# Experts in pairs, and their rows fetched by indirect DMA instead of gathered by one-hot products

## The chip, the core and the metric

The kernel runs on one core of one Trainium2 chip. The metric is the device time of one execution in microseconds, taken as the median of three runs.

## What is computed

One decoder layer on 512 tokens of 1024 channels in float32: a pooling mixer and multi-head latent attention side by side, an output projection, then a mixture of 32 experts of which each token takes four, and a final norm. The change lies in the mixture:

```python
logits = ht @ w_router + b_router
top_vals, top_idx = lax.top_k(logits, 4)
gates = jax.nn.softmax(top_vals, axis=-1)
...
gu = xblk @ w_gate_up[e] + b_gate_up[e]          # 1024 -> 2048
gate = jnp.minimum(gu[:, :1024], 7.0)
up = jnp.clip(gu[:, 1024:], -7.0, 7.0)
act = gate * jax.nn.sigmoid(1.702 * gate) * (up + 1)
return act @ w_down[e] + b_down[e]               # 1024 -> 1024
...
y = zeros.at[row_tok].add(row_gate[:, None] * yb)
```

All weights of all experts have to be read: 8 MB of gate-and-up and 4 MB of down for each of the 32.

## The kernel before

The first part (projections, attention, mixer, router) ends after about 200 us. Then the experts are worked on at 32 positions, ordered by how many tokens they have, in the pattern `KINDS = "BSSS" + "BS" * 12 + "SSSS"`. A big position (B) takes up to 128 tokens; its weights are split by `split` (L863) into a high part on ACT (L866) and a low part on DVE or POOL (L867), and each product is three passes (`mm3`, L95 to L97, for gate and up; L970 for down). A small position (S) takes up to 64 tokens and multiplies in float32 with two column halves side by side (L910, L992).

For each position the kernel does these steps: `load_expert` puts the weights into a ring of eight 1 MB slots by DMAs on SP's queue, in the order in which positions are worked on (8 slots of gate-and-up, then 4 of down). `select` (L794) makes a one-hot of the position's tokens over its slots on DVE. `gather` (L807) multiplies the normalised rows, kept in two float16 parts `hb`, with that one-hot (L837): 64 matmuls for a position, of 128 columns for B and of 64 for S, whose result already lies with channels on partitions. It is scaled into `xgs` (L848, S), or into `xgh` and `xgl` (L819 and L820, B). `gate_up` (L878) does the products, `act` the activation (`swiglu`, L917, on DVE and ACT), `turn` (L935) transposes it on PE (L949), `slot_info` (L850) gets token number and gate of every slot by the one-hot (L856), `down` (L958) does the second product, and `combine` (L1040) adds the gated rows to the tokens by scatter products (L1051) that a later `gate_up` takes along, one part after each of its steps.

The loop at L1278 runs position after position: gate-and-up of r, activation, the gather for r + 1, turn, down of r. The order on each engine's queue is not quite the program's: a scheduler in the framework lists the instructions of each engine by its own estimate of when they can run, and each engine then works through its list in order. In the list of PE the gate-and-up products of an S stand mixed with the down products of the B before it. PSUM has four banks `gu` for gate-and-up, two banks `d` for down and for half of a gather, and two banks `m` for the rest.

## Time and profile before

| | us |
|---|---|
| time, median of 3 runs (lowest, highest) | 1401.42 (1400.72, 1401.83) |
| profiled execution, first to last instruction (span) | 1392.6 |
| median time less that span | 8.8 |
| PE busy in the span | 1305.3 (94%) |
| DVE busy | 869.9 (62%) |
| ACT busy | 568.8 (41%) |
| POOL busy | 402.1 (29%) |

The profiled execution's own time is not listed apart from its span; what lies around the span is taken as the 8.8 us by which the median exceeds it. PE is the matmul engine, PEld its weight loads, DVE, ACT and POOL the vector, scalar and general engine, SP the engine whose queue issues the weight loads. A busy PE need not be PE at its peak, since matmuls overlap and their ends are modelled. The whole chain of waits is 62% PE. The mean granted clock of PE is 0.974 of 2.4 GHz.

### The profile page before, as it was taken

The numbers are of one execution on the slowest core, as the hardware profiler recorded it, in microseconds if no ns is written. First come the engines' busy times: TensorE is split into PE (matmuls) and PEld (weight loads), VectorE is DVE, ScalarE is ACT, GpSimd is POOL, SyncE is SP. The second block draws the span as 40 slices with busy tenths as digits, with TensorE's granted clock in tenths as the row PEclk, the third lists the DMA queues.
The fourth block names the chain that finished last, engine by engine and source line by source line (L and its number), as shares of the span: only waits on it lengthen the run. The fifth ranks groups of instructions, "written<-read, shape, count | busy, mean of one in ns | idle before, by whom it ended". The sixth has DMA issues, their size and how long they took to land.

```text
span 1392.6 us, 20172 instructions
## 1 busy us (share of the span) xinstructions
PE 1305.3 (94%) x7465; PEld 793.2 (57%) x7465; DVE 869.9 (62%) x1439; ACT 568.8 (41%) x819; POOL 402.1 (29%) x264
## 2 busy tenths in 40 slices
PE   7989988999899999999899999999899999999995
PEld 6756675534547465665657565746566565743432
DVE  6897688334847485675758593748577575832324
ACT  5476554212525263444434452626344444420003
POOL 1445334101514133332323241423333233310001
PEclk9999999999899999999999999999999999999998
DMA  8213417899889797979899898979797989999893
GB/s 300 76 59 105 155 73 257 332 407 373 327 333 334 276 382 274 378 289 367 327 333 355 335 338 320 356 293 380 273 385 287 369 326 359 346 351 399 343 421 138
DMA packets 83265, 422.29 MB, mean 303 GB/s; under 512 B 8729, under 2 KB 8857, under 8 KB 50394
## 3 DMA queue, kind: packets, MB, share of 16 engines
q1 hardware_dynamic: 82964, 420.57, 78.7%
q8 instruction: 60, 0.98, 0.3%
q10 hardware_dynamic: 198, 0.39, 0.1%
q14 instruction: 43, 0.35, 0.1%
HBM read 418.70 MB, written 2.23 MB: 302 GB/s over the span
## 4 chain that ended last, share of the span: by engine, by line
PE 62%; DVE 7%; ACT 2%; issue 1%; DVEq 0%; ACTq 0%
PE gu L910 18%; PE d L970 10%; PE d L992 7%; PE gu L95 5%; PE gu L96 5%; PE gu L97 5%; PE m L1051 5%; PE m L837 3%; DVE mlo L867 2%; DVE au L928 1%; PE m L949 1%; PE d L837 1%; DVE au L927 1%; ACT mhi L866 1%; DVE au L929 1%
## 5 line engine op out<-in xcount | busy, mean ns | idle before, releaser
L867 POOL TENSOR_TENSOR mlo<-slot,mhi 128x1024 fp32r<-128x1024 f32 x116 | 318.1, 2747 | 708.0 <-ACT mhi L866 707.9
L867 DVE TENSOR_TENSOR mlo<-slot,mhi 128x1024 fp32r<-128x1024 f32 x196 | 344.8, 1770 | 97.7 <-ACT mhi L866 95.4
L866 ACT CAST mhi<-slot 128x1024 fp32r<-128x1024 f32 x312 | 320.4, 1051 | 200.2 <-PE gu L97 133.2
L910 PE MATMUL gu<-slot,xgs 128*64 128x512 f32 x1216 | 305.8, 620 | 3.2 <-DVE xgs L848 3.2
L910 PEld LDWEIGHTS gu<-slot,xgs 128*64 128x64 f32 x1216 | 82.9, 140 | 151.7 <-issue 144.2
L96 PE MATMUL gu<-mlo,xgh 128*128 128x512 f32 x416 | 165.8, 399 | 2.9 <-DVE mlo L867 2.7
L97 PE MATMUL gu<-mhi,xgl 128*128 128x512 f32 x416 | 163.0, 393 | 0.0
L992 PE MATMUL d<-slot,ats 128*64 128x512 f32 x576 | 132.6, 609 | 0.0
L95 PE MATMUL gu<-mhi,xgh 128*128 128x512 f32 x416 | 127.5, 397 | 0.0
L926 ACT ACTIVATE as<-ag 128x512 f32<-128x512 f32 x45 | 28.4, 632 | 230.1 <-DVE ag L925 229.9
L837 PEld LDWEIGHTS <-hb 128*128 128x128 f16 x1984 | 83.2, 98 | 62.6 <-issue 62.1
L1052 DVE TENSOR_TENSOR y<-y,m 128x512 f32<-128x512 f32 x112 | 74.9, 681 | 48.0 <-PE m L1051 47.5
L925 DVE TENSOR_SCALAR ag<-gu 128x512 f32<-128x512 f32 x45 | 30.9, 688 | 115.9 <-PE gu L910 107.5
L96 PEld LDWEIGHTS gu<-mlo,xgh 128*128 128x128 f32 x416 | 78.3, 189 | 21.4 <-DVE mlo L867 4.0
L97 PEld LDWEIGHTS gu<-mhi,xgl 128*128 128x128 f32 x416 | 78.5, 189 | 16.1
L95 PEld LDWEIGHTS gu<-mhi,xgh 128*128 128x128 f32 x416 | 76.8, 188 | 18.1 <-issue 1.6
L992 PEld LDWEIGHTS d<-slot,ats 128*64 128x64 f32 x576 | 39.9, 139 | 73.7 <-issue 72.8
L977 DVE SCALAR_TENSOR_TENSOR ybl<-d,sl,ybh 128x512 fp32r<-128x512 f32 x26 | 18.3, 747 | 94.4 <-ACT ybh L976 94.4
L837 PE MATMUL m<-oh,hb 128*128 128x64 f16 (+1 forms) x1600 | 74.9, 200 | 1.0 <-DVE oh L802 0.9
L970 PE MATMUL d<-mhi,ath 128*128 128x512 f32 x208 | 69.4, 415 | 0.3 <-ACT ath L952 0.3
L970 PE MATMUL d<-mhi,atl 128*128 128x512 f32 x208 | 66.7, 401 | 0.0
L970 PE MATMUL d<-mlo,ath 128*128 128x512 f32 x208 | 66.2, 398 | 0.0
(389 smaller groups left out, 1687.8 us busy)
## 6 DMA issues: line engine op xcount, KB each, us to landing
slot<-in_w_gate_up_dram SPq DMA_DIRECT2D x256, 1024.0 KB, 6.9
slot<-in_w_down_dram SPq DMA_DIRECT2D x128, 1024.0 KB, 7.9
wraw<-in_w_in_dram SPq DMA_DIRECT2D x16, 256.0 KB, 5.0
wraw<-in_w_out_dram SPq DMA_DIRECT2D x16, 256.0 KB, 2.6
xtraw<-in_xT_dram SPq DMA_DIRECT2D x8, 256.0 KB, 5.1
y<-in_x_dram SPq DMA_DIRECT2D x4, 512.0 KB, 7.0
out_dram<-o SPq DMA_DIRECT2D x4, 512.0 KB, 2.6
wraw<-in_w_qb_dram SPq DMA_DIRECT2D x4, 256.0 KB, 3.5
```

The lines of the kernel that those rows point to most:

```text
L95: nc.tensor.matmul(out, lhsT=shi, rhs=mhi, start=first, stop=False)
L96: nc.tensor.matmul(out, lhsT=shi, rhs=mlo, start=False, stop=False)
L97: nc.tensor.matmul(out, lhsT=slo, rhs=mhi, start=False, stop=last)
L837: PE.matmul(pb[:, i * n:(i + 1) * n], lhsT=q[:, d * P:(d + 1) * P], rhs=oh[:, t, 0:n], start=(m == 0), stop=(m == len(ops) - 1))
L866: S.copy(hi, src)
L867: eng.tensor_tensor(lo, src, hi.bitcast(F32), op=ALU.subtract)
L910: PE.matmul(banks[c // 2][q:q + 64, :], lhsT=xg[r][:, k, :], rhs=w[:, c * T:(c + 1) * T], start=False, stop=(k == KD - 1))
L925: V.tensor_scalar(g, gb, 7.0, None, op0=ALU.min)
L970: PE.matmul(banks[c], lhsT=a[:, k, :], rhs=b[:, c * T:(c + 1) * T], start=(k == 0 and n == 0), stop=(k == KD - 1 and n == 2))
L992: PE.matmul(db[64 * q:64 * q + 64, :], lhsT=at[:, k, :], rhs=w[:, c * T:(c + 1) * T], start=(k == 0), stop=(k == KD - 1))
L1051: PE.matmul(pb, lhsT=a, rhs=b, start=(i == 0), stop=(i == len(todo) - 1))
L1052: V.tensor_tensor(y[:, t, cs], y[:, t, cs], pb, op=ALU.add)
```

## The change

Three things change together. First, the normalised rows are also written to DRAM (`hrow`, 512 rows of 4 KB, by eight DMAs on POOL's queue, `row_parts`). For a position, `fetch` turns the token numbers of its slots into an index column and issues one indirect DMA on POOL's queue, which brings 128 rows of 4 KB into `xr`, one row to a slot. An S and the S after it (`mate`) share one fetch. Second, `gather` turns `xr` by eight PE transposes of 128x128 for a B or for a pair of S's; the gather products at L837 are gone for all positions but the first. Third, the loop goes by a list of steps: after the first six positions, gate-and-up of two positions (a B and an S, at the end two S's), then both down products. The ring is loaded in the order of that list. Since the activation of the first of a pair has to outlive the next gather, `ath` and `atl` get buffers of their own, and PSUM is now six banks `gu` (down too) and two banks `m`. The other parts (`fetch` four steps ahead, `gather` two steps ahead for a B and one for S's, turn, combine) are generators from which `gate_up` and `down` take a part at each of their steps. In `row_parts` the low float16 part of the first token tile moves from POOL to DVE, and POOL makes the float32 rows. Line numbers move: in the changed kernel L849 is the transpose of the fetched rows, L919 and L1001 are the products of S, L959 is the transpose of the activation, L979 the down product of B, L1058 the scatter products, L865 the slot info, L876 the low part of a split.

```diff
-            if (t, c) in POOLP:
-                part = scr("part")
-                G.tensor_scalar(part, yt, r_, None, op0=ALU.mult)
-                G.tensor_tensor(hb[1][:, t, cs], part, hb[0][:, t, cs], op=ALU.subtract)
-            else:
-                V.scalar_tensor_tensor(hb[1][:, t, cs], yt, r_, hb[0][:, t, cs], op0=ALU.mult, op1=ALU.subtract)
+            V.scalar_tensor_tensor(hb[1][:, t, cs], yt, r_, hb[0][:, t, cs], op0=ALU.mult, op1=ALU.subtract)
+            part = cst.tile([P, T], F32, tag="xk3", name="part3") if t == NT - 1 and c else scr("part")
+            G.tensor_scalar(part, yt, r_, None, op0=ALU.mult)
+            G.dma_start(hrow[t * P:(t + 1) * P, cs], part)
...
+    def fetch(r):
+        idx = mo.tile([P, 1], I32, tag="idx", bufs=2, name="idx")
+        if big(r):
+            V.tensor_scalar(idx, slots[r][:, 5:6], 0.0, None, op0=ALU.max)
+        else:
+            q = mate(r)
+            V.tensor_scalar(idx[0:64], slots[r][0:64, 5:6], 0.0, None, op0=ALU.max)
+            V.tensor_scalar(idx[64:P], slots[r if q is None else q][64:P, 5:6], 0.0, None, op0=ALU.max)
+        rows[r] = hbp.tile([P, D], F32, tag="hb", name="xr")
+        G.indirect_dma_start(out=rows[r], out_offset=None, in_=hrow,
+                             in_offset=bass.IndirectOffsetOnAxis(ap=idx[:, 0:1], axis=0), bounds_check=T - 1,
+                             oob_is_err=False)
...
-        for b in range(nb):
-            pb = bank("d" if b and r != "o" and not big(r - 1) else "m")
-            for i in range(per):
-                d = b * per + i
-                ops = [(q[t], t) for t in range(NT) for q in src]
-                for m, (q, t) in enumerate(ops):
-                    PE.matmul(pb[:, i * n:(i + 1) * n], lhsT=q[:, d * P:(d + 1) * P], rhs=oh[:, t, 0:n],
-                              start=(m == 0), stop=(m == len(ops) - 1))
+        xr = rows.pop(r)
+        for b in range(2):
+            pb = bank("m")
+            for i in range(4):
+                d = 4 * b + i
+                PE.transpose(pb[:, i * P:(i + 1) * P], xr[:, d * P:(d + 1) * P], ident)
...
+    steps = [("gu", 0), ("dn", 0), ("gu", 1), ("gu", 2), ("dn", 1), ("gu", 3), ("dn", 2), ("gu", 4), ("dn", 3),
+             ("gu", 5), ("dn", 4), ("dn", 5)]
+    for r in range(6, E, 2):
+        steps += [("gu", r), ("gu", r + 1), ("dn", r), ("dn", r + 1)]
...
+    for i, (what, r) in enumerate(steps):
+        if i:
+            while loaded < i + 3:
+                load(loaded)
+                loaded += 1
+        ahead = {g: steps.index(("gu", g)) - i for g in groups}
+        for g, n in ahead.items():
+            if n <= (2 if big(g) else 1) and g not in gathered and i > 0:
+                gathered.add(g)
+                gathering = itertools.chain(gathering, later(gather(g), 5 if g == 1 else 1))
+            if n <= 4 and g not in fetched and i > 0:
+                fetched.add(g)
+                arriving = itertools.chain(arriving, arrive(g))
+        if what == "gu":
+            banks = gate_up(r, rest, turned, arriving, gathering)
...
+            us_ = act(r, banks)
+            turned = turn(r, us_)
...
+            down(r, rest, turned, arriving, gathering)
```

How the lists of the engines change is seen at three places. The first is on PE, where the last gate-and-up products of a B end. Before, the list goes on with bias products (L885), then the transposes of B's activation (L949, `au` is the activation, `m` a PSUM bank):

```order
L888 LDWEIGHTS m4b
L888 MATMUL gu<-bias,m4b 64x512
L885 LDWEIGHTS m4b
L885 MATMUL gu<-bias,m4b 128x512
L949 MATMUL m<-ident,au 128x128 x4
L885 LDWEIGHTS m4b
L885 MATMUL gu<-bias,m4b 128x512
L856 LDWEIGHTS oh
```

and with the change, at the same place:

```order
L919 MATMUL gu<-slot,xgs 64x512 x4
L96 MATMUL gu<-mlo,xgh 128x512
L97 MATMUL gu<-mhi,xgl 128x512
L96 MATMUL gu<-mlo,xgh 128x512
L97 MATMUL gu<-mhi,xgl 128x512
L919 MATMUL gu<-slot,xgs 64x512 x4
L959 MATMUL m<-ident,au 128x128 x4
L1058 MATMUL m<-ybh,sc 128x512
L1058 MATMUL m<-ybl,sc 128x512
L919 MATMUL gu<-slot,xgs 64x512 x4
L959 MATMUL m<-ident,au 128x128 x4
```

The transposes of the activation now stand behind products of the S of the pair (L919), which are ready to run, and no gather stands ahead of those.

The second place is on PE too, where B's down products run. Before, the S's gate-and-up products (L910) stand among them:

```order
L910 MATMUL gu<-slot,xgs 64x512 x8
L970 MATMUL d<-mhi,ath 128x512 x2
L970 MATMUL d<-mlo,ath 128x512 x2
L970 MATMUL d<-mhi,atl 128x512 x2
...
L949 MATMUL m<-ident,au 128x128 x4
...
L910 MATMUL gu<-slot,xgs 64x512 x8
```

With the change the S's products come first, with the transposes of a fetched group (L849) among them, and the down products of B (L979) follow:

```order
L919 MATMUL gu<-slot,xgs 64x512 x4
L849 MATMUL m<-ident,xr 128x128 x8
L919 MATMUL gu<-slot,xgs 64x512 x12
L979 MATMUL gu<-mhi,ath 128x512 x2
L959 MATMUL m<-ident,au 128x128 x4
```

The S's gate-and-up products, which filled the gaps between B's down products, now lie ahead of them.

The third place is POOL's list in the pairs, which before held only the splits' low parts after the start:

```order
L1180 MEMSET mblk 64x64
L1212 MEMSET aux 128x32 x4
L1249 MEMSET movb 64x64
L1156 TENSOR_TENSOR bd<-bdraw,bd 32x512 x2
L867 TENSOR_TENSOR mlo<-slot,mhi 128x1024 x115
```

and now has the fetches among them:

```order
L876 TENSOR_TENSOR mlo<-slot,mhi 128x1024 x9
L820 DMA xr<-hrow,idx 128x1024
L876 TENSOR_TENSOR mlo<-slot,mhi 128x1024 x4
L820 DMA xr<-hrow,idx 128x1024
L876 TENSOR_TENSOR mlo<-slot,mhi 128x1024 x5
```

Each fetch stands ahead of four, five or nine low parts, which POOL reaches only once it has issued the fetch.

## Rows read from the trace of the kernel before

**Rows 1.** The page's busy time, share of the span and instructions of each engine.

```profile
PE 1305.3 (94%) x7465; PEld 793.2 (57%) x7465; DVE 869.9 (62%) x1439; ACT 568.8 (41%) x819; POOL 402.1 (29%) x264
```

**Rows 2.** Chain of waits, S's down products of eleven pairs: start us, us, what.

```profile
492.14 5.30 PE d L992 x24
...
1242.46 7.02 PE d L992 x32
```

**Rows 3.** Windows, the ten pairs between: busy us (count) by engine, PEclk, DMA share, GB/s.

```profile
core 0: us, PE busy (x) PEld busy (x) DVE busy (x) ACT busy (x) POOL busy (x), PEclk, DMA share, GB/s
492.00:1242.00 750.00, 722.97 (x4208) 454.42 (x4207) 500.77 (x668) 329.55 (x415) 242.00 (x90) 0.98 0.88 336
```

**Rows 4.** Groups by line, activation's transposes: busy us, mean ns | idle before, releaser.

```profile
L949 PE MATMUL m<-ident,au 128*128 128x128 f32 x180 | 30.9, 298 | 28.6 <-DVE au L929 28.6
```

**Rows 5.** Windows, the first six positions.

```profile
209.00:420.00 211.00, 198.66 (x1181) 105.12 (x1179) 118.70 (x189) 66.05 (x86) 48.75 (x17) 0.97 0.87 338
280.00:310.00 30.00, 29.13 (x182) 12.24 (x184) 11.87 (x24) 3.90 (x6) 0.00 (x0) 1.00 1.00 406
340.00:370.00 30.00, 28.01 (x174) 19.87 (x170) 23.99 (x16) 18.36 (x19) 17.29 (x6) 1.00 0.97 373
```

**Rows 6.** Windows, the last four positions up to the tail.

```profile
1242.00:1355.00 113.00, 106.68 (x623) 39.61 (x623) 30.07 (x64) 9.90 (x16) 0.00 (x0) 0.97 0.96 387
1320.00:1340.00 20.00, 18.48 (x121) 6.68 (x119) 5.54 (x12) 1.22 (x2) 0.00 (x0) 1.00 1.01 427
```

**Rows 7.** Chain of waits: eight S products, B's gather in two halves, S's gather.

```profile
611.70 1.87 PE gu L910 x8
...
713.47 1.73 PE m L837 x29
715.19 1.79 PE d L837 x32
...
1238.63 1.94 PE m L837 x63
```

**Rows 8.** Timeline of PE: start us, us, instruction [idle before, releaser].

```profile
610.27 0.66 PE L949 MATMUL m<-ident,au 128*128 128x128 f32 x4 [1.47 <-DVE au L929]
...
642.82 0.61 PE L949 MATMUL m<-ident,au 128*128 128x128 f32 x4
643.26 0.60 PE L885 MATMUL gu<-bias,m4b 96*128 96x512 bf16 x2
```

**Rows 9.** The page's DMA issues: count, KB each, us to landing.

```profile
slot<-in_w_gate_up_dram SPq DMA_DIRECT2D x256, 1024.0 KB, 6.9
slot<-in_w_down_dram SPq DMA_DIRECT2D x128, 1024.0 KB, 7.9
```

**Rows 10.** Groups by line: the splits' low part on DVE and POOL.

```profile
L867 DVE TENSOR_TENSOR mlo<-slot,mhi 128x1024 fp32r<-128x1024 f32 x196 | 344.8, 1770 | 97.7 <-ACT mhi L866 95.4 <-DMA slot<-in_w_gate_up_dram 1.6
...
L867 POOL TENSOR_TENSOR mlo<-slot,mhi 128x1024 fp32r<-128x1024 f32 x116 | 318.1, 2747 | 708.0 <-ACT mhi L866 707.9
```

**Rows 11.** Groups by line: the low float16 part of the rows on DVE.

```profile
L607 DVE SCALAR_TENSOR_TENSOR hb<-y,r2s,hb 128x512 f16<-128x512 f32 x6 | 5.7, 968 | 0.8 <-ACT hb L601 0.8
```

**Rows 12.** Timeline of POOL while the row parts are made.

```profile
178.92 3.13 POOL L604 TENSOR_SCALAR part<-y,r2s 128x512 f32<-128x512 f32 x2 [10.72 <-DVE r2s L90]
182.02 2.73 POOL L605 TENSOR_TENSOR hb<-part,hb 128x512 f16<-128x512 f32 x2
...
191.85 0.14 POOL L1180 MEMSET mblk<- 64x64 f32 x1 [6.59 <-DMA slot<-in_w_gate_up_dram]
```

**Rows 13.** Groups by line: two DVE forms of 128x512, two inputs and one.

```profile
L929 DVE TENSOR_TENSOR au<-au,as 128x512 f32<-128x512 f32 x45 | 30.8, 685 | 1.7
...
L979 DVE TENSOR_SCALAR sc<-iota_t,sl 128x512 fp32r<-128x512 f32 x13 | 6.3, 483 | 0.0
```

**Rows 14.** Groups by line: evacuation of a scatter product's bank.

```profile
L1052 DVE TENSOR_TENSOR y<-y,m 128x512 f32<-128x512 f32 x112 | 74.9, 681 | 48.0 <-PE m L1051 47.5
```

More of the change, by code (lines that the diff above doesn't have):

```diff
@@ L1 @@
+import itertools
 from contextlib import ExitStack
@@ L127, in col @@
         return cols[:, c:c + 1]
+    dr = ctx.enter_context(tc.tile_pool(name="dr", bufs=1, space=DRAM))
+    hrow = dr.tile([T, D], F32, name="hrow")
     phase_a = ExitStack()
@@ L911, in gate_up @@
                               start=False, stop=(k == KD - 1))
-            next(rest, None)
+            for v in beside:
+                next(v, None)
         if r == 0:
@@ new lines, in block_kernel, with arrive, load @@
+    groups = {}
+    for r in range(1, E):
+        if big(r):
+            groups[r] = [r]
+        elif KINDS[:r].count("S") % 2 == 0:
+            groups[r] = [r] + [q for q in (mate(r),) if q is not None]
+    def arrive(r):
+        for q in groups[r]:
+            select(q)
+            yield
+            slot_info(q)
+        fetch(r)
+    def load(i):
+        if i >= len(steps):
+            return
+        what, r = steps[i]
+        if r == 0:
+            return
+        if what == "gu":
+            ev = nc.sync.value_load(eid[0:1, r:r + 1], min_val=0, max_val=E - 1)
+            load_expert(r, ev)
+        else:
+            load_down(r, wdown[r], r == E - 1)
@@ L1326, in block_kernel @@
+    assert not waiting
     rt.close()
```

191 lines of the change are left out of this document (91 added, 100 removed).

## The prediction

> **What bounds the kernel now.** I read the page's busy times first: PE is busy for 1305.3 of 1392.6 us [rows 1], no other engine for more than 62%. A mean hides stages, so the next view is the chain of waits, where the down products of each S mark the pace: from 492.14 to 1242.46 us there are ten periods of a B and an S, 75.03 us each [rows 2]. Ten more would look the same; this stretch is over half of the time. In it PE is busy for 722.97 of 750 us, so it idles 2.7 us a pair, while DVE is at 67% and the DMA engines at a share of 0.88, moving 336 GB/s [rows 3]. What PE waits for there is told by one group: the transposes of the activation wait 28.6 us in all for DVE's last activation step [rows 4]. So the pairs are bound by the amount of PE work, with a small wait at each activation.
>
> Two stretches differ. In the first six positions (209 to 420 us) PE is busy for 198.66 of 211 us and DMA has a share of 0.87; within it the weights come at 406 GB/s with a share of 1.00 for 30 us [rows 5]: there, with three S's in a row, weights and PE are about level. In the last four positions the DMA share is 0.96 over 113 us and reaches 1.01 at 427 GB/s [rows 6]: S after S, the weights set the pace, and PE's work there is free.
>
> **The change part by part.** The sum is made against the profiled execution: span 1392.6 us and 8.8 us around it, which I take from the median of 1401.42; the other runs lie within 0.8 us of that.
>
> *Gather to transposes.* A B's gather shows 61 of its 64 matmuls in 1.73 + 1.79 us, so 3.7 us; an S's shows 63 of 64 in 1.94 us, so 2.0 us [rows 7]. A pair gives up 5.7 us of PE. It gains eight transposes for the B and half of eight for the S, twelve. The activation's transposes are of the same form: four of them hold the next product off from 642.82 to 643.26 us, 0.44 us [rows 8]; twelve cost 1.3 us. Net 4.4 us a pair. PE is nearly gapless in this stretch, so all of it counts: eleven pairs (6 and 7 up to 26 and 27) give 48 us. The scaling out of PSUM (ACT, DVE) keeps its amount.
>
> *The pairs' order.* Before, PE's list puts the activation's transposes directly behind the last bias products, and they wait, 1.47 us in one instance [rows 8]. In the new list S products stand ahead of them in two places, eight of the trace's each time, 1.87 us [rows 7]. That can take away at most the 2.7 us of idle time and at worst nothing, since other waits may come: DVE's splits for the down products, at 1.77 us each [rows 10], no longer have an S's products beside them. I take 2.0 us, nearer to the upper end because the wait on DVE is most of the idle time and the list shows work in its place: 22 us over eleven pairs, bounds 0 and 30.
>
> *The weights.* A pair reads 24 MB-slots [rows 9], 25.2 MB, which is also 336 GB/s by 75.0 us [rows 3]. The fetches add 128 rows of 4 KB for the B and half of that for the S, 0.79 MB. At the 406 GB/s of a saturated window [rows 5] 26.0 MB take 64.0 us. My pair is 75.0 - 4.4 - 2.0 = 68.6 us, so the DMA share would rise to some 0.93 and stay hidden; the ring's eight slots, 2.6 us each, cover the uneven use within a pair. The Trainium skill, page "DMA: Bandwidth & Descriptors", section Specifications, speaks against this: it puts the limit of HBM for one core at about 358 GB/s, by which a pair could not be under 72.5 us and the sum would be some 43 us worse. The trace disagrees: 406 and 427 GB/s in windows of 30 and 20 us [rows 5, 6].
>
> *The first six positions.* PE work falls by three S gathers and a B's beside a further S's, 4 x 2.0 + 3.7 us, and rises by 24 transposes, 2.6 us: 9.1 us. PE idles 12.3 us there. The lower bound of the gain is 0, since weights are level with PE in part of it; the upper is 9 + 12 = 21 us. The new order also puts the first down product directly behind its own activation, with nothing beside it, where some 3 to 5 us may be lost. I take 12.
>
> *The last four positions.* Bound by weights [rows 6], so less PE work gains nothing. Two fetches for pairs add 0.52 MB each, 1.3 us at 406 GB/s: 2.6 us lost. Bounds 0 and 5.
>
> *Rows to DRAM.* DVE makes two more low parts, 0.97 us each [rows 11], in a stretch where it is nearly always busy: 2 us on the way to the first product. POOL makes eight float32 parts at 1.6 us [rows 12] and issues eight DMAs instead of two such parts and two subtractions; it waited 6.59 us just behind that place [rows 12], so that is hidden. The bounds are 0 and 6.
>
> *The fetches.* 22 indirect DMAs are issued by POOL. The trace of before shows no such operation. From below they cost nothing: POOL waits 708.0 us for ACT among its splits [rows 10], and a row's index is computed half a pair or more ahead of its transposes, 30 us and up, against a landing of 6.9 us for a 1 MB load among the others [rows 9]. From above, one takes POOL as long as a split, 2.75 us, and PE waits for all of it: 22 x 2.75 = 60 us. I take 0, the value nearest to POOL's idle time; the 60, 1384 us, lies just outside the range below.
>
> *Sum.* -48 - 22 - 12 + 2.6 + 2 = -77 us: span 1315, time 1324 us. The bounds on one side (0 for the order, 0 in front, 5 at the end, 6 for the rows) give 1364; those on the other (30, 21, 0, 0) give 1302. Changes of 0.2%, about 3 us, are what a measurement here can tell from none.
>
> **The rivals.**
>
> *The order gains nothing or costs.* Before, the scheduler already lays the S's products among the B's down products; the pairing may be there in all but name. With the change only two banks `m` are left for transposes, slot info, turns and scatter products, whose evacuation by DVE takes 0.68 us [rows 14] in a queue with splits of 1.77 us. If one such wait a step or two in a pair uses up the 2 us and 1 to 2 more, the pair is 71.7 us or so: 1324 + 11 x 3 = 1357, up to 1380 if the front gains nothing either. For it: DVE at 67% in the pairs. Against it: the chain shows hardly any wait for `m` now.
>
> *The weights become the bound.* At the 373 GB/s that one window shows at a share of 0.97 [rows 5], a pair takes 26.0 / 0.373 = 69.6 us, which gives 1335, still within the forecast. If besides the fetched rows hold the engines for twice their bytes, it is 26.8 / 0.373 = 71.8 us and 1324 + 11 x 3.2 = 1359. For it: a ring of eight slots has little in hand if the share comes near 1. Against it: 406 and 427 GB/s were reached [rows 5, 6]. At the limit that the Trainium skill's page "DMA: Bandwidth & Descriptors" gives, it would be 1324 + 11 x 3.9 = 1367.
>
> *Slower: PE stands at the fetched rows.* PE takes its list in order, so a transpose of a row that has not landed stops everything behind it. The same holds for POOL: a fetch that waits for its index stops the low parts behind it, which PE needs within some microseconds. The gain is 77 us over 22 fetches, so the point from which this decides is 3.5 us of PE a fetch. If PE waits a whole landing of 6.9 us [rows 9] at each, 22 x 6.9 = 152 us are lost, 1324 + 152 = 1476. For it: four, five or nine low parts stand behind every fetch. Against it: the lead of 30 us. The Trainium skill, page "SBUF — State Buffer", the box on DVE blocking a DMA in the section "SBUF: two separate sides", says that descriptors of a POOL DMA cannot be written while DVE runs an operation in a two-port mode, and gives 3.1 us in place of 0.62 us. By that 22 fetches cost 68 us at most. The trace lets such modes be guessed at: a one-input form takes 483 ns where a two-input one of the same size takes 685 [rows 13], but these are short and a small part of DVE's time.
>
> **How the numbers follow.** The forecast (1300 to 1345) gets 0.66: PE's work in the pairs is a sure thing and nothing else is near its limit. The order that gains nothing (1345 to 1380) gets 0.20, weights as the bound (around 1359) 0.05, PE at the fetched rows 0.09, of which 0.02 falls on no change and the rest on slower than before. So faster 0.91, same 0.02, slower 0.07. The range for 8 in 10 reaches over the forecast, somewhat below it (should pairs come near the 64 us that weights allow), and over most of the second case: 1288 to 1372.
>
> **What would show it.** Right: the S's down products of the pairs come every 68 to 69 us; PE's transposes L849 are twelve a pair, with no wait for a DMA before them; the waits of L959 for DVE are small; the DMA share in the pairs is 0.92 to 0.95 at some 375 GB/s, with PE over 97% busy. Wrong: PE waits for `xr` or for POOL's low part; gate-and-up products waiting for `slot` loads in the pairs; PE idle by over 4 us a pair, at an `m` bank.

## The result: 1415 us, 1.1% slower, where 1324 us was predicted

The changed kernel takes 1415.24 us (median of 4 runs, 1412.74 to 1417.08) and the kernel before, beside it on the same chip, 1401.07 us: ratio 1.0115, 95% interval 1.009 to 1.014. The time lies outside the range of 1288 to 1372 us and on the other side of no change.

The page's busy times of the changed kernel:

```profile
span 1412.7 us, 16684 instructions
PE 1271.1 (90%) x5657; PEld 735.4 (52%) x5657; DVE 923.4 (65%) x1482; ACT 568.6 (40%) x819; POOL 447.2 (32%) x298
```

PE has 34 us less to do than in [rows 1] and the span is 20 us longer. Cut at the same places in both traces, the 20 us lie as follows: up to the first expert product +7.0 (it starts at 207.1 us, before at 200.1), from there to the end of the S's down products at position 7 -6.4, the ten pairs up to the same place at position 27 +23.2, the end -3.6. So the loss is in the pairs. The windows view of them, with the columns of [rows 3] (stretch, length, busy time by engine, PEclk, DMA share, GB/s):

```profile
500.50:1273.20 772.70, 707.75 (x3037) 412.87 (x3035) 540.82 (x678) 326.83 (x410) 267.80 (x103) 0.96 0.90 336
```

772.7 us for ten pairs against 749.5. PE is idle for 772.7 - 707.8 = 64.9 us of them, before for 27.3 (27.0 in the stretch of [rows 3]), and the granted clock is 0.96 in place of 0.98: 61.4 us stood at the lower level, 1.2 GHz, before 30.7. A matmul lasts up to twice as long there, so about half of those 61.4 us is lost. PE's work at 2.4 GHz is then 707.8 - 30.7 = 677 us, before 722.2 - 15.4 = 707. The change took 30 us of work out of the ten pairs and put 38 us of waiting and 15 us of lost clock in.

The list of waits says for what (engine and line waited for, us in all, times, longest), over 492 to 1242 us:

```profile
PE gu L979 <- ACT mhi L875: 15.3, 9, 1.8
PE gu L96 <- DVE mlo L876: 9.7, 7, 2.2
PE gu L979 <- POOL mlo L876: 9.7, 13, 1.7
PE gu L979 <- DVE mlo L876: 7.1, 4, 1.8
PE m L849 <- DVE sl L867: 6.5, 4, 2.6
PE gu L96 <- POOL mlo L876: 6.4, 5, 1.9
```

and of the same list of the kernel before, the largest wait and the only one for a part of a split:

```profile
PE m L949 <- DVE au L929: 16.7, 9, 3.5
PE gu L96 <- DVE mlo L867: 0.4, 1, 0.4
```

The transposes of the activation, the large wait of [rows 4], are gone from the top. In their place PE waits 32.1 us at the B's down products (L979) for the split of their weights, and 16.1 us at the B's gate-and-up products (L96) for low parts. No line names `xr`: no transpose waits for fetched rows to land. The 6.5 us at L849 are for a bank `m`, which DVE first has to empty of slot numbers (L867). One pair as PE's timeline has it, from the end of the S's gate-and-up on:

```profile
624.96 1.94 PE L919 MATMUL gu<-slot,xgs 128*64 128x512 f32 x8
628.75 0.74 PE L979 MATMUL gu<-mhi,ath 128*128 128x512 f32 x2 [1.85 <-ACT mhi L875]
...
631.50 1.22 PE L979 MATMUL gu<-mlo,ath 128*128 128x512 f32 x2 [0.65 <-POOL mlo L876]
632.51 1.05 PE L979 MATMUL gu<-mhi,atl 128*128 128x512 f32 x2
...
638.08 0.63 PE L979 MATMUL gu<-mhi,ath 128*128 128x512 f32 x2
```

A wait of 1.85 us, another of 0.65 us, and then two products take 1.05 us in place of 0.63 until 637.6 us: the clock. The same place on ACT's timeline:

```profile
615.32 0.59 ACT L962 CAST ath<-m 128x512 fp32r<-128x512 f32 x1 [2.79 <-PE m L959]
622.61 0.37 ACT L833 ACTIVATE xgh<-m,gs 128x128 fp32r<-128x128 f32 x1 [6.71 <-PE m L849]
...
627.66 1.98 ACT L875 CAST mhi<-slot 128x1024 fp32r<-128x1024 f32 x2
```

ACT stands idle for 6.71 us, until PE has turned the next B's rows (L849), does their splits, and only then casts the down weights (L875). The chain of waits has their load landing at 612.7 us, 15 us earlier. The down products of a B, 11 us of PE work (48 products, two every 0.46 us), take 21.1 us in the mean of the ten pairs from first to last; before they took 17.9, with S products between them.

POOL's list shows one more reason. Another pair, on POOL, with the cast that its third low part needs, and on PE:

```profile
789.01 6.00 POOL L876 TENSOR_TENSOR mlo<-slot,mhi 128x1024 fp32r<-128x1024 f32 x2 [27.02 <-ACT mhi L875]
796.26 1.76 POOL L820 DMA_INDIRECT xr<-hrow,idx  x1 [1.26 <-DVE idx L814]
798.05 5.78 POOL L876 TENSOR_TENSOR mlo<-slot,mhi 128x1024 fp32r<-128x1024 f32 x2
```

```profile
793.89 1.05 ACT L875 CAST mhi<-slot 128x1024 fp32r<-128x1024 f32 x1 [1.21 <-issue]
```

```profile
800.55 0.73 PE L979 MATMUL gu<-mlo,ath 128*128 128x512 f32 x2 [1.67 <-POOL mlo L876]
```

On DVE, the next fetch's one-hots and index in between its low parts:

```profile
793.02 2.66 DVE L798 TENSOR_SCALAR oh<-iota_s,posm 128x128 f16<-128x128 f32 x4
795.84 0.14 DVE L814 TENSOR_SCALAR idx<-sl 128x1 int32<-128x1 f32 x1
```

The cast ends at 794.94 us and POOL is free at 795.01. But a fetch stands ahead in POOL's list: POOL waits 1.26 us for the index and takes 1.76 us to issue, the low part starts 3.0 us late, and PE waits 1.67 us for it. Of the 17.6 us that PE waits for POOL's low parts in the ten pairs, 11.4 us, in ten waits, are for a low part that starts directly behind a fetch.

### The profile page after: what moved, and what is told of

Its sections match the earlier page's. It is cut to its first block, busy times and chain, and to the rows that moved or that the text cites. A ratio compares the mean times of both kernels' runs of the same rounds, so it can differ in the third digit from the quotient of the medians.

```text
span 1412.7 us, 16684 instructions
## 1 busy us (share of the span) xinstructions
PE 1271.1 (90%) x5657; PEld 735.4 (52%) x5657; DVE 923.4 (65%) x1482; ACT 568.6 (40%) x819; POOL 447.2 (32%) x298
## 4 chain that ended last, share of the span: by engine, by line
PE 35%; issue 14%; DVE 5%; DMA 5%; POOL 4%; ACT 1%; POOLq 0%; DVEq 0%; ACTq 0%
PE gu L919 7%; PE gu L979 5%; PE gu L1001 5%; DMA slot<-in_w_down_dram 4%; PE gu L96 4%; PE gu L97 4%; PE gu L95 4%; POOL mlo L876 4%; DVE mlo L876 3%; PE m L1058 3%; DMA slot<-in_w_gate_up_dram 1%; ACT mhi L875 1%; PE m L849 1%; POOL xr L820 1%; PE gu L1036 1%
## 5 line engine op out<-in xcount | busy, mean ns | idle before, releaser
L876 POOL TENSOR_TENSOR mlo<-slot,mhi 128x1024 fp32r<-128x1024 f32 x116 | 316.8, 2737 | 586.8 <-ACT mhi L875 584.9
L876 DVE TENSOR_TENSOR mlo<-slot,mhi 128x1024 fp32r<-128x1024 f32 x196 | 350.8, 1817 | 40.9 <-ACT mhi L875 39.8
L875 ACT CAST mhi<-slot 128x1024 fp32r<-128x1024 f32 x312 | 317.6, 1049 | 148.8 <-PE gu L97 95.1
L919 PE MATMUL gu<-slot,xgs 128*64 128x512 f32 x1216 | 284.2, 600 | 2.2 <-DMA slot<-in_w_gate_up_dram 2.2
L96 PE MATMUL gu<-mlo,xgh 128*128 128x512 f32 x416 | 168.6, 405 | 19.7 <-DVE mlo L876 10.9
L919 PEld LDWEIGHTS gu<-slot,xgs 128*64 128x64 f32 x1216 | 79.3, 136 | 154.9 <-issue 147.2
L1001 PE MATMUL gu<-slot,ats 128*64 128x512 f32 x576 | 139.9, 617 | 2.8 <-DMA slot<-in_w_down_dram 2.1
L1059 DVE TENSOR_TENSOR y<-y,m 128x512 f32<-128x512 f32 x120 | 81.0, 683 | 78.4 <-PE m L1058 77.2
L936 ACT ACTIVATE as<-ag 128x512 f32<-128x512 f32 x45 | 28.4, 631 | 235.0 <-DVE ag L935 235.0
L96 PEld LDWEIGHTS gu<-mlo,xgh 128*128 128x128 f32 x416 | 79.2, 190 | 52.4 <-DVE mlo L876 16.9
L979 PE MATMUL gu<-mlo,ath 128*128 128x512 f32 x208 | 78.7, 463 | 24.4 <-POOL mlo L876 16.4
L979 PE MATMUL gu<-mhi,ath 128*128 128x512 f32 x208 | 73.3, 436 | 21.1 <-ACT mhi L875 20.4
L820 POOL DMA_INDIRECT xr<-hrow,idx x22 | 33.8, 1536 | 143.7 <-DVE idx L818 80.5
L1001 PEld LDWEIGHTS gu<-slot,ats 128*64 128x64 f32 x576 | 37.4, 139 | 75.6 <-issue 67.0
L979 PE MATMUL gu<-mhi,atl 128*128 128x512 f32 x208 | 72.5, 433 | 0.0
L1014 DVE SCALAR_TENSOR_TENSOR ysl<-gu,sl,ysh 64x512 fp32r<-64x512 f32 x36 | 26.9, 748 | 67.1 <-ACT ysh L1012 66.6
L986 DVE SCALAR_TENSOR_TENSOR ybl<-gu,sl,ybh 128x512 fp32r<-128x512 f32 x26 | 18.3, 746 | 78.4 <-ACT ybh L985 78.4
```

The source lines that it names most:

```text
L96: nc.tensor.matmul(out, lhsT=shi, rhs=mlo, start=False, stop=False)
L820: G.indirect_dma_start(out=rows[r], out_offset=None, in_=hrow, in_offset=bass.IndirectOffsetOnAxis(ap=idx[:, 0:1], axis=0), bounds_check=T ...
L875: S.copy(hi, src)
L876: eng.tensor_tensor(lo, src, hi.bitcast(F32), op=ALU.subtract)
L919: PE.matmul(banks[c // 2][q:q + 64, :], lhsT=xg[r][:, k, :], rhs=w[:, c * T:(c + 1) * T], start=False, stop=(k == KD - 1))
L979: PE.matmul(banks[c], lhsT=a[:, k, :], rhs=b[:, c * T:(c + 1) * T], start=(k == 0 and n == 0), stop=(k == KD - 1 and n == 2))
```

## The experiments

18 kernels ran. Columns: median, ratio to the kernel before on the same chip; then for the ten pairs their length, PE's idle time and the time at 1.2 GHz, counted from the same two places in each trace.

| | us | ratio [95%] | pairs | idle | 1.2 GHz |
|---|---|---|---|---|---|
| before | 1401.07 | 1 | 749.5 | 27.3 | 30.7 |
| changed | 1415.24 | 1.0115 [1.009, 1.014] | 772.7 | 64.9 | 61.4 |
| e0 before, rows to DRAM | 1391.99 | 0.9968 [0.9952, 0.9983] | 740.6 | 27.2 | 13.7 |
| e1 before, rows fetched | 1432.93 | 1.0261 [1.0236, 1.0286] | 769.8 | 65.6 | 71.7 |
| e2 pairs, gathers | 1413.30 | 1.0130 [1.0105, 1.0155] | 763.4 | 30.2 | 20.5 |
| e3 changed, splits early | 1415.67 | 1.0154 [1.0123, 1.0184] | 775.7 | 65.0 | 68.3 |
| e6 e1 + idle products | 1476.76 | 1.0547 [1.0503, 1.0592] | 805.9 | 32.2 | 54.6 |
| e7 changed + idle products | 1450.06 | 1.0350 [1.0304, 1.0395] | 781.4 | 34.3 | 23.9 |
| e4 changed, rows later | 1388.53 | 0.9919 [0.9889, 0.9950] | 749.8 | 54.6 | 37.5 |
| e8 e4, low parts last | 1370.29 | 0.9787 [0.9743, 0.9832] | 733.2 | 46.3 | 10.2 |
| e9 e8 with gathers | 1425.01 | 1.0197 [1.0174, 1.0220] | 779.2 | 37.5 | 23.9 |
| e10 before, low parts last | 1378.43 | 0.9856 [0.9832, 0.9881] | 733.6 | 21.5 | 13.7 |
| e11 e8, low last in gate-and-up too | 1367.21 | 0.9779 [0.9742, 0.9816] | 729.8 | 43.6 | 13.7 |
| e12 e1, low parts last | 1440.96 | 1.0310 [1.0288, 1.0333] | 776.1 | 65.5 | 85.3 |
| e13 e1, masks late | 1417.58 | 1.0125 [1.0097, 1.0153] | 765.7 | 56.8 | 68.3 |
| e14 e11, masks late | 1441.54 | 1.0290 [1.0244, 1.0335] | 796.7 | 89.2 | 75.1 |
| e15 changed, masks late | 1433.30 | 1.0242 [1.0215, 1.0268] | 790.5 | 80.2 | 68.3 |
| e16 e11, down splits on DVE | 1349.70 | 0.9648 [0.9631, 0.9665] | 715.3 | 37.6 | 13.7 |
| e17 e11, all splits on DVE | 1331.70 | 0.9519 [0.9502, 0.9536] | 708.2 | 33.6 | 0.0 |
| e18 e10, down splits on DVE | 1394.09 | 0.9964 [0.9947, 0.9982] | 750.5 | 28.5 | 23.9 |

### The parts of the change by themselves: e0, e1, e2

e0 is the kernel before with the rows written and nothing read:

```diff
+            V.scalar_tensor_tensor(hb[1][:, t, cs], yt, r_, hb[0][:, t, cs], op0=ALU.mult, op1=ALU.subtract)
+            part = cst.tile([P, T], F32, tag="xk3", name="part3") if t == NT - 1 and c else scr("part")
+            G.tensor_scalar(part, yt, r_, None, op0=ALU.mult)
+            G.dma_start(hrow[t * P:(t + 1) * P, cs], part)
```

> The kernel before, with one part of the change added: all low parts on DVE, and the eight f32 half-rows of the normalised tokens made on POOL and written to DRAM by POOL's queue. Nothing reads them. Theory 1 (the write delays the start): in the profile of the changed kernel gate-and-up of position 0 began 7.0 us later than before (207.1 against 200.1 us), behind eight POOL products of 1.55 to 1.85 us and eight DMA issues of 0.57 us; so 1401 + 7 = 1408 us (1405 to 1412). Theory 2 (the delay of the start came from the changed order, not from the write): 1401 us (1399 to 1404).

The first expert product comes 5.0 us later (205.1 us), so that part of theory 1 holds, but the whole is 5 us faster, below both ranges: 17 us less at 1.2 GHz in the ten pairs give back more. Writing the rows is no loss. The edit lies ahead of the pairs, and still they are 8.9 us shorter: the scheduler's lists of PE, ACT and DVE came out in another order there too. So a difference of some 9 us in the pairs is not by itself the work of an edit.

e1 keeps the old loop and fetches each position's rows two positions ahead:

```diff
-                    PE.matmul(pb[:, i * n:(i + 1) * n], lhsT=q[:, d * P:(d + 1) * P], rhs=oh[:, t, 0:n],
...
+                PE.transpose(pb[:, i * n:(i + 1) * n], xr[0:m, d * P:(d + 1) * P], ident[0:m, 0:m])
...
+        if r + 2 < E:
+            arrive(r + 2)
```

> The order of the work as before, one position after another; the rows are written to DRAM, fetched by indirect DMA two positions ahead and transposed on PE, no one-hot gathers. Theory 1 (the pairs' order is what costs, the fetched rows are worth what PE is spared): PE is spared 34 us in the two profiles (1305.3 to 1271.1 us), the prediction took 48; with 7 us for the write of the rows this gives 1401 - 34 (or 48) + 7 = 1360 to 1374 us. Theory 2 (the fetched rows cost, since the splits of their columns come late on ACT and DVE, or since the fetch slows DVE): no gain, 1400 to 1415 us.

Both theories fall; it is 36 us slower. PE's work in the pairs is down to 769.8 - 65.6 - 35.9 = 668 us, 39 less than before, but the idle time grew by 38 us. PE's timeline at the end of a B's gate-and-up:

```profile
632.14 0.71 PE L832 MATMUL m<-ident,xr 64*128 64x64 f32 x8
633.32 0.41 PE L892 MATMUL gu<-bias,m4b 96*64 96x512 bf16 x2 [0.48 <-DVE ag L929]
635.18 0.41 PE L892 MATMUL gu<-bias,m4b 96*64 96x512 bf16 x2 [1.45 <-DVE au L931]
635.78 0.38 PE L889 MATMUL gu<-bias,m4b 96*128 96x512 bf16 x1 [0.19 <-DVE au L931]
639.64 1.12 PE L953 MATMUL m<-ident,au 128*128 128x128 f32 x4 [3.49 <-DVE au L933]
640.69 3.68 PE L914 MATMUL gu<-slot,xgs 128*64 128x512 f32 x8
```

PE waits for DVE's activation, and the eight S products behind it take 3.68 us; in [rows 7] eight take 1.87.

e2 is the changed kernel with the one-hots and gathers back and no fetch.

> The changed kernel's order in pairs, but with the one-hot gathers of before (two rows' one-hots made just ahead of their gather; POOL free of the rows' product, write and fetch). Theory 1 (the pairs' order costs): the pairs' 27 us over what fetched rows alone would give (changed kernel 77.3 us a pair against 75.0 - 4.4 = 70.6 predicted) stay, so 6.7 us x 11 to 12 pairs is lost against before: 1401 + 75 = 1476, less what gathers fill of the waits for the down splits; 1425 to 1480 us. Theory 2 (the order costs nothing, the fetch does): 1380 to 1401 us.

The order alone costs 16 us, less than theory 1's number and on the side that theory 2 excludes. The pairs are 13.9 us longer, hardly by idle time (30.2 against 27.3 us): 14.7 us of waits for the down splits and 11.8 us for banks `m` have taken the place of the 16.7 us for the activation. PE's work at full clock is 723 us against 707, in matmuls of which most groups take somewhat longer (the products with the down weights' low part 432 ns in the mean against 397; S's gate-and-up, 602 against 632, is shorter). So neither part brings a gain alone, and together they lose what the order loses alone.

### The down splits: e3, e4, e8

e3 emits the first four splits of the B's down weights inside the S's gate-and-up.

> The changed kernel, with the first four splits of the B position's down weights issued on ACT, DVE and POOL during the S position's gate-and-up, ahead of the next B's rows in ACT's list. Theory 1 (PE waits at the B's down products because their splits start only after the S's gate-and-up, ACT standing behind the next B's rows): the B's down products take 17.6 to 24.5 us a pair against 11.4 us of PE work; they should take 12 to 15 us, the spells at half clock behind these waits (118.4 us in all) should shrink to 75 us or fewer, and the pair go from 77.3 to 70 to 73 us: 1415 - 11 x 5.5 = 1355 us (1340 to 1380). Theory 2 (the splits are late anyway, since DVE and POOL are what lacks, or the weights land late): the wait moves to the gate-and-up of the next B and the time stays, 1400 to 1418 us.

It tested nothing: the scheduler, whose estimate places the casts by when it takes the loads to land, put them back to the same place. In the pairs the lists of ACT, DVE and POOL are the changed kernel's, and so is the time. The ACT timeline, 2.3 us earlier:

```profile
620.30 0.37 ACT L833 ACTIVATE xgh<-m,gs 128x128 fp32r<-128x128 f32 x1 [6.71 <-PE m L849]
...
625.34 1.98 ACT L875 CAST mhi<-slot 128x1024 fp32r<-128x1024 f32 x2
```

e4 moves the other side, the next B's rows, behind:

```diff
-            if n <= (2 if big(g) else 1) and g not in gathered and i > 0:
+            if n <= 1 and g not in gathered and i > 0:
```

> The changed kernel with the transposes of the next B's rows one step later, so that ACT's list has the B's down splits ahead of those rows' splits (in ACT's list of instructions the first casts now stand ahead of the first row's cast). Theory 1 (the splits of the B's down weights start late because ACT's list has them behind the next B's rows): the B's down products go from 21.3 us in the mean to 17 or 18 us, the pair from 77.4 to 73 to 75 us, 1375 to 1395 us. Theory 2 (the splits wait for the activation of the S, which stands ahead of them in either list, or for POOL and DVE, and the rows are then late for the next gate-and-up): no change or slower, 1412 to 1430 us.

The numbers are theory 1's: 27 us faster than the changed kernel, the B's down products 17.8 us in place of 21.1, the pair 75.0. ACT's timeline has the casts ahead of the rows:

```profile
623.31 0.63 ACT L936 ACTIVATE as<-ag 128x512 f32<-128x512 f32 x1 [9.49 <-DVE ag L935]
623.85 1.98 ACT L875 CAST mhi<-slot 128x1024 fp32r<-128x1024 f32 x2
626.35 0.59 ACT L966 COPY ats<-m 128x512 f32<-128x512 f32 x1 [0.52 <-PE m L959]
626.83 0.37 ACT L833 ACTIVATE xgh<-m,gs 128x128 fp32r<-128x128 f32 x1
```

But they still come behind the S's sigmoid (L936), as theory 2 had it, and PE still waits 1.59 us for the first. Over the ten pairs its waits for ACT's casts hardly fell:

```profile
PE gu L979 <- ACT mhi L875: 15.9, 10, 1.6
```

against 16.9 us, also ten, in the changed kernel. What went are the waits at L979 for DVE's low parts (7.1 us), at L849 for slot numbers (6.5 us), and 6.3 of the 17.6 us for POOL's low parts, of which those behind a fetch fell from 11.4 to 0.8 us. For the edit also moved the fetch, and DVE's work on its one-hot and index, behind the B's low parts:

```profile
628.22 9.63 POOL L876 TENSOR_TENSOR mlo<-slot,mhi 128x1024 fp32r<-128x1024 f32 x3 [0.40 <-ACT mhi L875]
644.90 1.01 POOL L820 DMA_INDIRECT xr<-hrow,idx  x1 [7.05 <-DVE idx L814]
```

So e4 shows the place, the B's down products, and not that it was the rows in ACT's list; no run moves the rows or the fetch alone.

e8 changes besides the order of the three products of a step:

```diff
-                for n, (a, b) in enumerate(((hi, wh), (hi, wl), (lo, wh))):
+                for n, (a, b) in enumerate(((hi, wh), (lo, wh), (hi, wl))):
```

> The kernel with the rows later, and in the B's down products the order of the three products of a step changed: both that need the high part of the weights first, then the one that needs the low part. Theory 1 (PE waits at the low parts from POOL and DVE by 0.5 to 1.8 us a time, 17 us in the middle pairs): each low part gets 0.46 us more, so 5 to 10 us less than the kernel with the rows later alone, clock included. Theory 2 (the high parts from ACT are what comes last, so the low parts' lateness only moves): within 3 us of it.

18 us, twice what theory 1 gave: idle time fell by 8.3 us in the pairs and the time at 1.2 GHz from 37.5 to 10.2 us. Not where theory 1 had it, though: the waits for POOL's low parts at L979 stay (9.9 and 9.5 us) and the down products take 17.2 us against 17.8. What fell are the waits at L96 for DVE's low parts, 13.6 to 6.4 us. The lists of ACT and DVE changed with the edit, so its own share of the 18 us is open.

### Is it PE's work at all? e6, e7

As many float16 products as the gathers had, from a constant tile, ahead of the transposes, which overwrite their results:

```diff
+                for j in range(2 * NT):
+                    PE.matmul(pb[:, i * n:(i + 1) * n], lhsT=oh0[:, j % NT, :], rhs=oh0[:, (j + 1) % NT, 0:n],
+                              start=(j == 0), stop=(j == 2 * NT - 1))
```

> The kernel of the fetch alone (before's order, rows fetched and transposed, 1432.9 us), with as many float16 products as the gathers had put back ahead of the transposes, from a constant tile; their results are overwritten by the transposes, so they are work without a use. Theory 1 (the gathers cost nothing before, since they stood in PE's waits for DVE's activation and kept its granted clock up; the fetch itself is free): PE gets 56 us more to do in the ten middle pairs and yet the time falls, towards 1392 us (the rows written, gathers used) plus 17 us of transposes at most: 1392 to 1412 us, and the half-clock time falls from 161 to about 80 us. Theory 2 (the fetch, its index and slot work on DVE and POOL are what costs): the waits stay and the products come on top where they do not fit, 1433 to 1470 us.

> The changed kernel (1415 us) with the same products without a use ahead of its transposes. Theory 1 (PE's work is not what bounds the changed kernel; its waits for splits and the half clock behind them are): 56 us of PE work in the ten middle pairs change the time little, 1405 to 1425 us, with fewer waits and less half-clock time than 118 us. Theory 2 (the changed kernel is bound by PE's work, and its waits come on top of it): 1450 to 1475 us.

Theory 1 falls in both; e7 is at the lower edge of theory 2, e6 7 us above both of its ranges. In e6 PE's work in the pairs rises by 78 us (65 of it in the products) and the pairs by 36: what had been idle (33 us) and slow (9 us) took the rest. In e7 it is 58 of work, 31 of idle time, 19 of lost clock, and 9 us in the pairs, but 35 in all, of which 25 are in the first eight positions. So the gathers had filled waits, though not for nothing; PE's work is on the path, and the waits are on it too.

### Two by two: e9 to e12

e9 is e8 with gathers, e10 the kernel before with the one line of e8, e12 is e1 with it; e11 puts the low part last in gate-and-up too.

> The kernel with the rows later and the low parts last (1370 us), its fetch, transposes and rows in DRAM taken out again, the one-hot gathers back in their place. Theory 1 (with the waits gone the fetched rows are worth the PE work that they spare): gathers of 56.2 us against transposes of 14.6 to 18 us in the ten middle pairs, and the front's two S pairs: 1370 + 40 to 50 = 1410 to 1420 us. Theory 2 (the gathers only filled PE's waits, and the arrangement alone made the gain): 1365 to 1380 us.

> The kernel before with nothing changed but the order of the three products in the B's down products (low part of the weights last). Theory 1 (the low parts are late only in pairs, where the B's down products have nothing beside them; before, the S's products stood between): no change, 1394 to 1402 us. Theory 2 (the gain of 18 us belongs to any order): 1378 to 1386 us.

> The kernel with the rows later and the low parts last (1370 us), and the same order of the three products in the B's gate-and-up too. Theory 1 (PE still waits there at low parts, 8 us in 750, and each is wanted 0.23 us later now): 1360 to 1367 us. Theory 2 (DVE at 74% is the next bound, so that the wait moves): 1367 to 1374 us.

> The kernel of the fetch alone in before's order (1432.9 us) with the low parts last in the B's down products. Theory 1 (its loss lies at the waits for DVE's activation, 50 us in 750, not at the down splits): within 5 us of 1433. Theory 2 (any spared wait in the down products gives the clock back): 1410 to 1425 us.

e9: theory 1, and more. With waits out of the way the fetched rows are worth 1425.0 - 1370.3 = 55 us, 46 of them in the ten pairs. e10: theory 2. The order of the products is worth 1.4% to the kernel before as well, so of e8's gain over the old kernel most is not the change's. The kernel before has no wait at its down products in PE's list; e10 gains at the waits for the activation (16.7 to 10.9 us) and at 1.2 GHz (30.7 to 13.7 us), again with other lists of ACT and DVE, so how it comes by them is not shown. e11's 3 us lie on the border of its two theories and tell nothing. e12 is 8 us slower than e1, outside both, which speaks against the down splits as the place of the fetch's loss in the old order. In the old order the fetch loses 36 and 63 us, in the new one with its waits mended it gains 55.

### DVE's masks and POOL: e13 to e18

With the token numbers known early, the scheduler lets the scatter masks (`ss`, `sc`) go ahead of the activation on DVE. e13 to e15 hold them back behind it:

```diff
+    def pin(r, us_):
+        sl = mo.tile([P, 7], F32, tag="sl2", bufs=4, name="sl2")
+        V.scalar_tensor_tensor(sl[:, 5:7], us_[-1][:, 0:2], 0.0, slots[r][:, 5:7], op0=ALU.mult, op1=ALU.add)
+        slots[r] = sl
```

> The kernel of the fetch alone in before's order (1432.9 us), with the scatter masks held back: the slot numbers that they are made from go through one small DVE operation behind the position's activation. In DVE's list the masks then stand behind the activation, as they did before. Theory 1 (an index that is known two positions ahead lets the masks, 0.5 to 2.1 us each, slip in front of the activation that PE waits for, 52 of its 66 idle us in the middle pairs): the waits and the half clock behind them fall to before's, 1433 to 1375 to 1400 us. Theory 2 (the activation is late for another reason, the gathers' gone work above all: PE comes to it sooner): within 8 us of 1433.

> The best so far (pairs, rows later, low parts last in both products, 1367 us) with the masks held back in the same way. Theory 1 (the masks delay activations in pairs too): 1350 to 1362 us. Theory 2 (in pairs the S's products stand between activation and turn, so PE does not wait there: its waits for au are 1.4 us in 750): 1363 to 1371 us.

> The changed kernel (1415 us) with the masks held back and nothing else. Theory 1 (the masks are part of its loss): 1385 to 1405 us. Theory 2 (its loss is at the down splits alone, which the rows one step later mended by 27 us): 1410 to 1420 us.

e13 falls between its theories: 15 of the 36 us went with the edit. e14 and e15 miss both of theirs, being 74 and 18 us slower than the same kernels without the edit, and show more than a hit would have. DVE's timeline in e14 at the place where the down splits are due:

```profile
635.76 0.69 DVE L942 TENSOR_TENSOR au<-au,as 128x512 f32<-128x512 f32 x1
636.49 2.22 DVE L973 SCALAR_TENSOR_TENSOR sl<-au,sl 128x2 f32<-128x2 f32 x1
638.75 5.06 DVE L1018 TENSOR_SCALAR ss<-iota_t,sl 64x512 fp32r<-64x512 f32 x2
643.84 2.36 DVE L876 TENSOR_TENSOR mlo<-slot,mhi 128x1024 fp32r<-128x1024 f32 x2
```

What POOL does meanwhile:

```profile
635.81 7.71 POOL L876 TENSOR_TENSOR mlo<-slot,mhi 128x1024 fp32r<-128x1024 f32 x3 [25.32 <-ACT mhi L875]
```

And PE's wait:

```profile
645.12 1.22 PE L987 MATMUL gu<-mlo,ath 128*128 128x512 f32 x2 [4.70 <-DVE mlo L876]
```

A DVE operation on 128x2 elements takes 2.22 us, two masks 5.06 us; the low part behind them is 4.70 us late for PE. Nearly all of it lies beside POOL's low parts, 635.81 to 643.52 us. The groups by line of e11 and e14 say that this is no single case (mean ns behind the busy time), e11 first:

```profile
L1013 DVE TENSOR_SCALAR ss<-iota_t,sl 64x512 fp32r<-64x512 f32 x36 | 17.3, 481 | 0.4
```

```profile
L1018 DVE TENSOR_SCALAR ss<-iota_t,sl 64x512 fp32r<-64x512 f32 x36 | 52.0, 1444 | 0.8
```

In e14 26 of the 36 masks run beside POOL for more than a fifth of their time and take 1.81 us in the mean; the other ten take 0.48 us.

And the mean of DVE's low parts, 1770 ns in [rows 10], hides two kinds. Sorted by whether POOL makes a low part during more than a fifth of them, the kernel before has 74 of 1.23 us and 122 of 2.10 us, the changed kernel 99 of 1.22 and 97 of 2.42. The Trainium skill, page "SBUF — State Buffer", section "Who interferes with whom", has the rule: a DVE operation with two inputs from SBUF, or one in a two-port mode, and an operation of GpSimd (POOL here) that reads SBUF exclude each other for the whole instruction. The trace agrees, with 1.22 against 2.42 us.

So the last three kernels take the low parts off POOL:

```diff
-                wh, wl = split(wslots[r, "dn", k, 0], G if k % 2 == 0 else V)
+                wh, wl = split(wslots[r, "dn", k, 0], V)
```

e16 is e11 with this line, e17 has the low parts of gate-and-up on DVE as well, e18 is e10 with the line.

> The best so far (pairs, rows later, low parts last, 1367 us) with all eight low parts of a B's down weights on DVE, none on POOL. In the traces a low part on DVE takes 1.23 us with POOL idle and 2.1 to 2.5 us beside one of POOL's. Theory 1 (the two engines keep each other from these operations, so that halving them between the two gains little and makes the first ones late): eight low parts take DVE 9.8 us in a down product of 17.2 us, PE's waits there for POOL and DVE (9.4 us in 750) go, the down products take 14 to 15.5 us, and the time is 1340 to 1358 us. Theory 2 (DVE, at 76% in the pairs, is the next bound and more work on it makes other things late): 1367 to 1395 us.

> As the last, with the low parts of the gate-and-up on DVE too, none on POOL. Theory 1: 312 low parts at 1.23 us are 384 us of DVE, against 351 us for 196 of them in the changed kernel, so DVE has hardly more to do: 1325 to 1355 us. Theory 2 (a low part every 1.6 us in the gate-and-up leaves DVE no room for its other work): 1367 to 1420 us.

> The kernel before with the low parts last in the down products (1378.4 us) and all eight of them on DVE. Theory 1 (the collision of DVE and POOL is there in any order): 1355 to 1372 us, so that this gain too belongs to both orders. Theory 2 (in the old order the S's products hide the late low parts, and DVE's activations come later): 1376 to 1395 us.

Theory 1 holds for e16 and e17: the B's down products take 15.1 to 15.4 us in each pair, and e17 at 1331.7 us is 4.8% faster than the kernel before. The busy times on its page:

```profile
PE 1231.2 (93%) x5657; PEld 719.0 (54%) x5657; DVE 889.5 (67%) x1598; ACT 561.3 (42%) x819; POOL 130.0 (10%) x182
```

Its group of low parts (busy us, mean ns, idle before):

```profile
L876 DVE TENSOR_TENSOR mlo<-slot,mhi 128x1024 fp32r<-128x1024 f32 x312 | 364.5, 1217 | 7.3 <-ACT mhi L875 5.8
```

DVE makes 312 low parts in place of 196 and is busy for 889.5 us, less than the 923.4 of the changed kernel. In the pairs no time at 1.2 GHz is left. With POOL out of the splits three things go at once: the collision, POOL's own 2.4 us for a low part, and the fetch that stood ahead of some; e16 and e17 do not tell their shares apart. The wait for ACT's first cast stays in both, 15.9 us in ten pairs. e18 is 16 us slower than e10, in theory 2's range: the old order does not gain by it; PE waits there for DVE's rows and low parts (15.5 and 6.0 us in 750). Only the down splits were moved there, so what e17's step would do to the old order stays open.

## Why the prediction was wrong

**The gather to transposes (-48 us): the size was right, the condition was not.** PE's work in the ten pairs is 723 us with gathers in pairs (e2) and 677 in the changed kernel, 4.6 us a pair where 4.4 were predicted. But the step said that all of it counts since PE is nearly gapless. From e2 to the changed kernel the time changed by 2 us: idle time in the pairs rose from 30.2 to 64.9 us and the time at 1.2 GHz from 20.5 to 61.4 us, which is 35 and 20 us against the 46 us of work that was spared. In e8 against e9, where the waits are fewer, all of it counts (46 us in the ten pairs).

**The pairs' order (-22 us, bounds 0 to -30): the step that failed.** The order alone costs 16 us (e2). For the ten pairs the two steps gave -64 us and the trace +23. Of these 87 us, 58 are idle time (38 us more, where 20 less were taken), 15 the clock and 14 PE's work (30 us less in place of 44). The prediction said "at worst nothing, since other waits may come", and named the very wait: DVE's splits, which "no longer have an S's products beside them". It gave it no price. What it missed is what else the engines do, in the order of their lists, between the last input and the low parts. ACT's first cast stands behind the S's sigmoid, DVE's low parts behind the S's activation and around the next fetch's one-hot and index, POOL's behind the fetch. With nothing beside the B's down products, each lateness there is PE's: 21.1 us for 11 us of work. The place is shown by e4 (17.8 us, the ten pairs 23 us shorter), e16 (15.4 us, 15 us shorter than e11) and, from the other side, e14 (23.6 us in place of e11's 17.2, the pairs 67 us longer).

**Durations from a mean.** The 1.77 and 2.75 us of [rows 10] were taken as they stood. Paired, four low parts on POOL and four on DVE are due at once, and DVE's that run beside POOL's take 2.42 us in the mean. e17, with none on POOL, has 1.22 us for all 312; how much of the changed kernel's loss this was is not shown apart from the fetch and POOL's own pace.

**The clock.** The sum had no term for it; 61 us at 1.2 GHz in the pairs against 31 cost 15 us. Every spell in the pairs of the kernel before, the changed kernel, e1 and e2 begins in or close behind waits of PE, 1.3 to 5.6 us in all, as in the timelines above; in e17 ten waits of 1.59 us, one a pair, are followed by none.

**Front, rows, end.** The first eight positions gained 6.4 us (predicted 12 for six of them, with bounds 0 and 21, and 6.4 for the pair behind them), the end gained 3.6 (predicted a loss of 2.6). The start lost 7.0 us where 2 were taken with a bound of 6; 5.0 of them come with the write alone (e0). The 8.8 us around the span were too many: the profiled run of the changed kernel took 1414.44 us for a span of 1412.7, so 1.7 us. That alone made the forecast 7 us too high.

**The fetches (0 us).** Right for the landing, not for POOL. PE never waits for `xr` to land in the changed kernel. But its waits behind POOL's fetches are 11.4 us in the ten pairs, 0.8 us for each of 14, and DVE's one-hot and index for them stand among the low parts; in e2, the same order without fetches, PE waits 1.8 us for POOL's low parts in place of 17.6. "PE waits for POOL's low part" and an idle PE of over 4 us a pair (6.5) were the prediction's own signs of being wrong. The page has 22 issues of 1.5 us on POOL:

```profile
L820 POOL DMA_INDIRECT xr<-hrow,idx x22 | 33.8, 1536 | 143.7 <-DVE idx L818 80.5
```

The weights were no bound either: e17 moves 369 GB/s in a window of its pairs at a share of 0.96, near the predicted 375.

**The rivals.** The first, that the order gains nothing or costs, came true in kind: its price was 1357 to 1380 and its place a bank `m`, where PE waits 11.3 us in 750 (6.3 before), so about 0.5 us a pair more. The slower case named PE at the fetched rows, which did not happen, and low parts stopped behind a fetch that waits for its index, which did, at less than a third of the 3.5 us a fetch from which it would decide alone. No rival had the down splits late by more than the whole gain.

**What stays open.** Of the 36 us that the fetch alone costs in the old order, 15 went with e13's edit; the rest is waits for DVE's activation whose cause was not tried. The 16 us of e2 sit in longer matmuls whose cause was not traced further. Whether the rows in ACT's list or the fetch made the changed kernel's down splits late, e4 does not tell. The wait for ACT's first cast behind the S's sigmoid, 15.9 us in ten waits in e4, e8, e11, e16 and e17, was left as it is.

With the rows later, the low parts last and POOL out of the splits, the change comes to 1331.7 us. That this is 8 us from the forecast is luck: POOL out of the splits was no part of the sum, and the low parts last are worth 18 us to the kernel before too. What e8 and e9 show is that the fetched rows can be worth the PE work that they spare, once the waits are fewer.

## What to carry to other kernels

Before counting PE's saved work as time, go to the place where two stages now meet without overlap and list for each engine what must be done between the last input and the first matmul, in the order of its own queue; price that gap, even at a bound. Look at the distribution of a duration behind its mean, beside which other engine's work it is long: an operation shared out to POOL can cost DVE more than it takes off it. And when a change "does nothing", move the suspected neighbour rather than the suspect, since a scheduler may put the suspect back; then compare the lists of all engines, because the edit may have moved more than the neighbour.

## What the runs showed of the hardware

POOL's and DVE's two-input float32 operations of 128x1024 slow each other: in the changed kernel DVE takes 1.22 us alone and 2.42 beside POOL, POOL 2.43 alone and 2.81 beside DVE. A DVE operation with one input from PSUM is not slowed: `y<-y,m` on 128x512 takes 0.69 us alone and beside POOL. A DVE mask of 64x512 takes 0.48 us alone and 1.81 beside POOL in e14, and an operation on 128x2 elements took 2.22 us there. An indirect DMA of 128 rows of 4 KB took POOL 1.54 us in the changed kernel, 1.17 to 1.22 in e4 and e8, 1.51 in e17. In the pairs of the kernel before, the changed kernel, e1 and e2 waits of PE of 1.3 to 5.6 us in all were followed by a granted clock of 1.2 GHz for 3.4 to 10.2 us: e1's pairs have 39 us less work than before and 38 us more waiting, and are 20 us longer by the clock alone.
